# Fifteen seven-product pairs a layer, a middle convolution tap split between ScalarE and adding transfers, a down projection in four parts and a sixth split-weight slot, in a two-layer hybrid decoder on one core

## The chip, the cores and the metric

The kernel runs on one core of a Trainium2 chip. The metric is device time in microseconds (us), the median of several runs, lower is better. In the profile, PE is TensorE's matmul stream and PEld its weight loads, DVE is VectorE, ACT is ScalarE, POOL is GpSimd, and SP is the queue that issues most transfers. Lines are those of the kernel before; most instructions carry line 189, that of the helper through which all of them are recorded, so that groups are told apart by tile names.

## The reference, cut to what matters

Two layers (`DEPTH = 2`) over `x` of 512 tokens by 1024 channels, all in float32. Each layer mixes tokens (a convolution module, block-sparse attention and gated linear attention, side by side, under one input projection `w_in` and one output projection `w_out`), and then runs a gated MLP with a causal convolution of width 3 inside it:

```python
h = rms_norm(x, norm_ffn_g[l])                                  # 512 x 1024
u = causal_depthwise_conv(h @ ffn_w_up[l], ffn_conv_w[l], ffn_conv_b[l])   # 512 x 5632
x = x + (jax.nn.silu(u[..., :2816]) * u[..., 2816:]) @ ffn_w_down[l]       # 2816 -> 1024
```

The change lies almost wholly in this MLP. The output is `rms_norm(x, final_g)`.

## The kernel before

**How a product is done.** Activations lie transposed: 128 channels on the partitions, 512 tokens along them, so `x_sb[m]`, m = 0 to 7, are eight tiles of 128x512. A float32 product is made of three matmuls of split operands (`mm3`, line 458): high by high, high by low, low by high. Weights come raw from memory (`wraw`, issued by `dma_piece`, line 347, on SP, with three raw buffers), and are split on the chip by `split_piece` (line 367): ACT copies the rounded high part to `whi`, DVE subtracts it to give `wlo`. Split weights lie in `NWB = 5` slots of 1088 columns, and `ahead` (line 433) begins the split of up to two pieces beyond the one in use.

**The MLP.** The 2816 hidden channels are 22 blocks of 128, j = 0 to 21; for each j there is a block of the gate half (half 0, which goes through silu) and one of the other (half 1). Up projections come in two kinds. An "up" unit makes one block of one half: 24 matmuls of 128x512. A "pair" (`pair_unit`, line 508) makes both blocks of one j at once, over token halves, by seven products in place of eight (Strassen's scheme in Winograd's form): 84 matmuls of 128x256, and in return sums of weights (`sums`, line 389, inside `split_piece`: four DVE additions, two more half-size splits) and six additions or copies of half tiles when the PSUM banks are emptied (`ffn_pair`, line 1474). The sums of activations that all pairs share are made once a layer (`operand_sums`, line 1522). `PAIRS` (line 59) names the j that are pairs: 8 to 21 without 15, thirteen a layer.

**The convolution.** `taps` (line 1448) takes a block `u` that lies in a padded buffer: ACT writes `t = u * fw(2) + bias`, DVE adds `u` shifted by one times `fw(1)`, then `u` shifted by two times `fw(0)`; for half 0 ACT applies silu; when both halves are there DVE multiplies them, and the product is split again into the operands `gT_[j]` of the down projection. The padded buffers come from `take_pad` (line 1429), which has POOL clear two columns first.

**The down projection** sums over the 22 blocks in `PARTS = [8, 8, 6]`: each part is eight units m = 0 to 7, each of 3 matmuls per block of the part. The result of a part that isn't the last goes through `residual_job` (line 781): ACT copies the PSUM bank into a temporary `t`, and POOL issues a transfer that adds it to `x_sb[m]` (`x<-t`, line 787). The last part ends the layer, and is added by DVE.

**What sets the order.** The program is one hand-run schedule. `ffn_plan` (line 70) lists the MLP's units: for each j two "up"s or one "pair", and `DPER = 2` down units after each j from the point where their part is due. All other work (splits, convolutions, evictions) is written as generators (`Job`), which yield the tiles that they wait for; `tick`, called between the matmuls, runs a job's next step when a `Clock` with a cost for each engine says that what it needs is ready, and `force` runs jobs until a condition holds. Each engine then takes its instructions in the order in which they were so emitted. A transfer that adds is given a fixed delay in this clock, before what it writes counts as ready (`DLAT = 8000`, in ns):

```python
nc.gpsimd.dma_start(out=x_sb[m], in_=t, accum_op=ALU.add)
clk.ready[key(x_sb[m])] = max(clk.ready.get(key(x_sb[m]), 0.0), clk.t["PE"]) + DLAT
```

The vb projection, by `unit_tok` (line 556), is the one place where activations are the stationary operand and weights, 272 columns wide, stream; its weights came in two pieces of 1088 columns. `gate` is a 96x512 pattern of ones and zeros, built once by POOL at the start (lines 671 and 677), and `columns` (line 772) makes a column of scales for the vb rows, using the identity `ident`.

Of the kernel before, what the change touches and what calls it, by code (L numbers as in the profile page):

```python
# [8 lines left out]
F32 = mybir.dt.float32  # L9
# [8 lines left out]
P = 128  # L18
# [9 lines left out]
PARTS = [8, 8, 6]  # L28
OFFS = [0, 8, 16]
VBW = 272  # L30
WSLOT = 4 * VBW
# [13 lines left out]
TB = 48  # L45
# [11 lines left out]
NWB = 5  # L57
H = S // 2
PAIRS = [j for j in range(8, 22) if j != 15]
DPER = 2  # L60
NRAWJ = 3
DLAT = 8000.0
Q = 4 * P
# [131 lines left out]
def trunk(ctx, tc, xT, wg, wi, wvb, wc, wo, wug, wuh, wu, ws, wdg, wd, cols, gatew, fing, outT):  # L195
# [119 lines left out]
    for l in range(DEPTH):  # L315
        pieces += [(wg[l, i], 2 * GW) for i in range(4)]
        tok = 0
        for names in PLAN[1:]:
            if names[0] == "vb":
                pieces += [(wvb[l, i], 4 * VBW) for i in range(2)]  # L320
            elif names[0] in WIDE:
                pieces += [(wc[l, tok + i], 2 * S) for i in range(4)]
                tok += 4
            else:
                pieces += [(wi[l, UNITS.index(names[0])], KD * P)]
        pieces += [(wo[l, i], KD * P) for i in range(8)]
        pieces += [(wug[l, i], 2 * GW) for i in range(4)] + [(wu[l, i], KD * P) for i in range(2 * NRAWJ - 3)]
        pieces += [(wuh[l, i], 2 * GW) for i in range(4)] + [(wu[l, 2 * NRAWJ - 3], KD * P)]
        nu = 2 * NRAWJ - 2
        for what, a, b in FFN:  # L330
            if what == "up":
                pieces += [(wu[l, nu], KD * P)]
                nu += 1
            elif what == "pair":
                i = PAIRS.index(a)
                pieces += [(ws[l, i, 0], 2 * Q, "first"), (ws[l, i, 1], 2 * Q, "second")]
            elif what == "down":
                o, n = OFFS[a], PARTS[a]
                pieces += [(wd[l, b, :, o * P:(o + n) * P], n * P)]
        o, n = OFFS[-1], PARTS[-1]  # L340
        pieces += [(wdg[l, :, a * GW:b * GW], (b - a) * GW) for a, b in pairs(n)]
        pieces += [(wd[l, m, :, o * P:(o + n) * P], n * P) for m in range(3, KD)]
    st = {"next": 0, "dma": 0, "split": 0, "live": 0, "held": 0, "q": 1}
    raws, loaded = {}, {}
    AHEAD = 2
# [87 lines left out]
    def ahead():  # L433

        while st["split"] < min(len(pieces), st["next"] + AHEAD):
            if st["live"] + (2 if pieces[st["split"]][2:] == ("second",) else 1) > NWB:
                break
            split_piece()
# [69 lines left out]
    def pair_unit(B, on_done):  # L508
# [11 lines left out]
        st["held"] += 2  # L520
        k4 = lambda t: t.rearrange("p (k c) -> p k c", c=P)
# [34 lines left out]
    def unit_tok(lhs, w, on_done):  # L556

        ws = get(2)
        hs = [a.rearrange("p (k c) -> p k c", c=w) for a, _ in ws]
        ls = [b.rearrange("p (k c) -> p k c", c=w) for _, b in ws]  # L560
        for tb in range(NT):
            ps = PM()
            sl = slice(tb * P, (tb + 1) * P)
            for k in range(KD):
                mm3(ps[:, :w], lhs[k][0][:, sl], lhs[k][1][:, sl], hs[k // 4][:, k % 4, :],
                    ls[k // 4][:, k % 4, :], k == 0, k == KD - 1)
            post(on_done(tb, ps), ps)
# [68 lines left out]
    ones = const.tile([P, P], F32, name="ones")  # L636
    V.memset(ones, 1.0)
    mean_f = const.tile([P, P], F32, name="mean_f")
# [11 lines left out]
    ident = const.tile([P, P], F32, name="ident")  # L650
    nc.gpsimd.memset(ident, 0.0)
    nc.gpsimd.affine_select(out=ident, in_=ident, compare_op=ALU.not_equal, fill=1.0, base=0,
                            pattern=[[-1, P]], channel_multiplier=1)
    identr = const.tile([P, P], F32R, name="identr")
    nc.gpsimd.tensor_copy(out=identr, in_=ident)
    cmaskf = const.tile([P, P], F32, name="cmaskf")
# [13 lines left out]
    gate_0 = const.tile([96, S], F32, name="gate_0")  # L670
    nc.gpsimd.memset(gate_0, 0.0)

    def gate_weights():
        yield lambda: max(2e4, clk.ready.get(key(gw_sb), INF))
        A.activation(gate_w.rearrange("p l c -> p (l c)"), gate_0, AF.Copy)
        for r in (16, 80):
            nc.gpsimd.affine_select(out=gate_0, in_=gate_0, compare_op=ALU.not_equal, fill=1.0, base=-r,
                                    pattern=[[0, S]], channel_multiplier=1)
# [120 lines left out]
    def last_blocks(ks):  # L799
# [23 lines left out]
        def half(m, hs):  # L823
            def f(ps):
# [14 lines left out]
                if m + 2 == KD:  # L839
                    yield [acc, 1]  # L840
                    stat[hs.start] = PX()
                    PE.matmul(stat[hs.start][:, :H], mean_f, acc[:, hs], start=True, stop=False)
                yield [sq]
                PE.matmul(stat[hs.start][:, :H], mean_f, sq[:, :H], start=False, stop=m + 1 == KD)
# [200 lines left out]
    def gla_gates(l, vb, kT, qT, res, flags, qbd):  # L1045
# [6 lines left out]
        A.activation(gT[:96], gate_0, AF.Copy)  # L1052
# [208 lines left out]
    for l in range(DEPTH):  # L1261
# [186 lines left out]
        def taps(half, j, u):  # L1448
# [5 lines left out]
                             bias=col_sb[:, l, C_FB + cj:C_FB + cj + 1])  # L1454
                yield [t]
                V.scalar_tensor_tensor(t, u[:, 1:1 + S], fw(1), t, op0=ALU.mult, op1=ALU.add)
                V.scalar_tensor_tensor(t, u[:, 0:S], fw(0), t, op0=ALU.mult, op1=ALU.add)
                pads["n"] += 1
# [114 lines left out]
        ks = lambda pi: gT_[OFFS[pi]:OFFS[pi] + PARTS[pi]]  # L1573
        for what, i, m in FFN:
# [4 lines left out]
            else:  # L1579
                unit(ks(i), res(i, m))  # L1580
        if l + 1 == DEPTH:
            last_blocks(ks(last))
            break
# [7 lines left out]
def _layout(x, norm_mix_g, w_in, conv_w, conv_b, conv_ln_g, conv_ln_b, moba_out_g,  # L1591
# [18 lines left out]
    wvb = np.concatenate(parts(vbw, 4), axis=1)  # L1610
# [51 lines left out]
```

## Time and profile before

| | |
|---|---|
| median of 3 runs | 1129.82 us (1129.62 to 1130.07) |
| profiled execution, its own time | 1129.47 us |
| span in that execution | 1127.8 us |
| mean granted TensorE clock, of full speed | 0.997 |
| busy share of the span: PE, DVE, ACT, POOL | 99%, 82%, 57%, 6% |
| mean traffic over the span | 106 GB/s |

The span is the time from the first to the last instruction on the core; 1.67 us of the execution lie around it. Shares of busy time are means over the span. A matmul's duration in the rows is longer than the distance from one to the next, since they are pipelined; what a stretch costs is read from starts. A row of a timeline that ends in x2 stands for two instructions in a row, and its time is that of both.

### The profile page before, as it was taken

What the parts mean: (1) busy time and instruction counts of PE and PEld (TensorE: products, weight loads), DVE (VectorE), ACT (ScalarE), POOL (GpSimd) and SP (SyncE); (2) the same over time, 40 slices, a digit from 0 to 9 for tenths busy, and PEclk for the clock granted to TensorE, in tenths of its full rate; (3) what the DMA queues carried; (4) which work ended last, traced back from release to release, by engine and by line L of the source; (5) the groups of instructions that cost most, each with busy time, mean ns of one, the idle gap of its engine ahead of it and who ended that gap; (6) DMA issues with size and microseconds to landing.
All of it is one profiled execution on the core that took longest, in us unless ns stands there. A gap on an engine that the chain in (4) does not pass through costs nothing.

```text
span 1127.8 us, 17164 instructions
## 1 busy us (share of the span) xinstructions
PE 1116.4 (99%) x6582; PEld 972.3 (86%) x6582; DVE 921.0 (82%) x1489; ACT 640.7 (57%) x1016; POOL 67.8 (6%) x181
## 2 busy tenths in 40 slices
PE   9999999999999999999999999999999999999996
PEld 6988888888899899998888878888889899999886
DVE  7998866799987789767779979567999878996764
ACT  7465764667554555544554576446666554564554
POOL 2000102000000000100000011010000010000000
PEclk9999999999999999999999999999999999999998
DMA  7322227233254433453332212262323354244432
GB/s 238 97 74 74 63 66 156 87 98 98 71 143 119 110 115 112 124 152 92 119 115 75 75 57 75 76 137 92 108 94 107 100 132 137 88 125 137 99 108 75
DMA packets 40036, 119.00 MB, mean 106 GB/s; under 512 B 4609, under 2 KB 6913, under 8 KB 39954
## 3 DMA queue, kind: packets, MB, share of 16 engines
q1 hardware_dynamic: 32210, 104.53, 29.8%
q0 software_dynamic: 6912, 12.59, 6.4%
q8 instruction: 51, 0.84, 0.3%
q10 hardware_dynamic: 832, 0.79, 0.2%
q14 instruction: 31, 0.25, 0.1%
HBM read 103.21 MB, written 2.10 MB: 93 GB/s over the span
## 4 chain that ended last, share of the span: by engine, by line
PE 98%; ACT 1%; DVE 0%; DMA 0%; issue 0%; ACTq 0%; DVEq 0%
PE pm L189 82%; PE px L189 16%; ACT t L189 0%; DMA g_sb<-in_dram 0%; DVE t L189 0%; ACT x L189 0%; DVE wlo L189 0%; ACT whi L189 0%; DVE x L189 0%; ACTq L611 0%; DVEq L1657 0%; DVEq L189 0%; ACTq L189 0%
## 5 line engine op out<-in xcount | busy, mean ns | idle before, releaser
L189 PE MATMUL pm<-t,whi 128*128 128x512 f32 (+1 forms) x2476 | 685.8, 362 | 0.8 <-ACT t L189 0.8
L189 PEld LDWEIGHTS pm<-t,whi 128*128 128x128 f32 x2476 | 441.0, 189 | 71.1 <-ACT t L189 1.6
L189 PE MATMUL pm<-t,wlo 128*128 128x512 f32 (+1 forms) x1238 | 443.7, 360 | 0.4 <-DVE wlo L189 0.4
L189 DVE TENSOR_TENSOR wlo<-wraw,whi 128x1024 fp32r<-128x1024 f32 (+4 forms) x229 | 252.6, 1109 | 61.6 <-ACT whi L189 61.3
L189 PEld LDWEIGHTS pm<-t,wlo 128*128 128x128 f32 x1238 | 233.7, 189 | 36.3 <-DVE wlo L189 0.9
L189 ACT ACTIVATE whi<-wraw 128x1024 fp32r<-128x1024 f32 (+3 forms) x227 | 218.8, 968 | 57.1 <-DMA wraw<-in_dram 32.2
L189 ACT ACTIVATE t<-t 128x512 f32<-128x512 f32 (+3 forms) x220 | 133.0, 618 | 151.9 <-DVE t L189 150.3
L189 DVE TENSOR_TENSOR t<-t 128x512 f32<-128x512 f32 (+3 forms) x219 | 139.7, 651 | 18.8 <-ACT t L189 16.5
L189 DVE SCALAR_TENSOR_TENSOR t<-u,col_sb,t 128x512 f32<-128x512 f32 x176 | 129.9, 749 | 14.5 <-ACT t L189 10.5
L189 PE MATMUL pm<-bop,whi 128*128 128x256 f32 x516 | 96.7, 283 | 0.0
L189 ACT ACTIVATE t<-u,col_sb 128x512 f32<-128x512 f32 x88 | 68.9, 809 | 34.4 <-DVE u L189 33.9
L189 DVE SCALAR_TENSOR_TENSOR t<-hp,col_sb,t 128x512 f32<-128x512 f32 x120 | 82.6, 744 | 2.8 <-issue 2.3
L189 PEld LDWEIGHTS pm<-bop,whi 128*128 128x128 f32 x516 | 80.5, 192 | 0.0
L189 PE MATMUL pm<-bop,wlo 128*128 128x256 f32 x258 | 73.2, 284 | 0.0
L189 PE MATMUL px<-t,whi 128*128 128x512 f32 (+1 forms) x244 | 73.1, 374 | 0.0
L189 ACT COPY t<-pm 128x512 f32<-128x512 f32 x70 | 40.5, 578 | 49.8 <-PE pm L189 49.3
L787 POOL DMA_DIRECT2D x<-t x48 | 41.9, 909 | 421.2 <-ACT t L189 372.0
L189 PE MATMUL pm<-whi,t 128*128 128x272 f32 (+1 forms) x224 | 59.3, 339 | 0.0
L189 PEld LDWEIGHTS px<-t,whi 128*128 128x128 f32 x244 | 44.6, 188 | 8.1
L189 PEld LDWEIGHTS pm<-bop,wlo 128*128 128x128 f32 x258 | 49.5, 192 | 0.1
L189 ACT COPY u<-pm 128x256 f32<-128x256 f32 (+1 forms) x48 | 22.3, 465 | 44.5 <-PE pm L189 44.5
L189 ACT COPY t<-px 128x512 f32<-128x512 f32 (+2 forms) x50 | 24.5, 507 | 38.3 <-PE px L189 36.2
(158 smaller groups left out, 1144.4 us busy)
## 6 DMA issues: line engine op xcount, KB each, us to landing
wraw<-in_dram SPq DMA_DIRECT2D x158, 512.0 KB, 3.6
wraw<-in_dram SPq DMA_DIRECT2D x39, 384.0 KB, 3.3
x<-t POOLq DMA_DIRECT2D x48, 256.0 KB, 5.3
wraw<-in_dram SPq DMA_DIRECT2D x4, 544.0 KB, 3.8
x<-in_dram SPq DMA_DIRECT2D x7, 256.0 KB, 5.6
out_dram<-t SPq DMA_DIRECT2D x4, 256.0 KB, 2.3
out_dram<-t SPq DMA_DIRECT2D x4, 128.0 KB, 2.2
out_dram<-t ACTq DMA_DIRECT2D x2, 256.0 KB, 2.2
```

Of the source, the lines that this page charges most:

```text
L189: return real(*a, **k)
L787: nc.gpsimd.dma_start(out=x_sb[m], in_=t, accum_op=ALU.add)
```

## The change

- `PAIRS` becomes j = 7 to 21, fifteen a layer (7 and 15 are new).
- The down projection has four parts, of 5, 5, 6 and 6 blocks.
- For j = 3 to 20 the middle tap leaves DVE: ACT writes `mid = u * fw(1)` of the shifted block into another temporary, DVE does the tap `fw(0)` first, and then POOL issues a transfer that adds `mid` to `t` (line 1468 of the changed kernel), after which `t` counts as ready 6000 ns later (`TLAT`). What read `t` before (silu, or the product) now waits for that transfer.
- There are six split-weight slots, of 1024 columns; in the MLP `ahead` looks three pieces ahead, and a pair calls it once more at its start. For this the vb weights come in three pieces (816, 816 and 544 columns), and small constants move into temporaries: the identity is used through its rounded copy, and the gate pattern is made by POOL anew in each layer (`gate_pattern`, a memset and two selects).

```diff
-PARTS = [8, 8, 6]
-OFFS = [0, 8, 16]
+PARTS = [5, 5, 6, 6]
+OFFS = [0, 5, 10, 16]
 VBW = 272
-WSLOT = 4 * VBW
+WSLOT = KD * P
+VPARTS = ((0, 3), (3, 6), (6, 8))
...
-TB = 48
+TB = 47
...
-NWB = 5
+NWB = 6
 H = S // 2
-PAIRS = [j for j in range(8, 22) if j != 15]
+PAIRS = [j for j in range(7, 22)]
 DPER = 2
 NRAWJ = 3
 DLAT = 8000.0
+TLAT = 6000.0
+TAPJ = range(3, 21)
...
-                pieces += [(wvb[l, i], 4 * VBW) for i in range(2)]
+                pieces += [(wvb[l, :, a * VBW:b * VBW], (b - a) * VBW) for a, b in VPARTS]
...
-        while st["split"] < min(len(pieces), st["next"] + AHEAD):
+        while st["split"] < min(len(pieces), st["next"] + st["ahead"]):
...
         quads, _ = loaded.pop(i)
         st["held"] += 2
+        ahead()
...
-        ws = get(2)
+        ws = get(len(VPARTS))
...
+    def gate_pattern():
+        t = T()[:96]
+        nc.gpsimd.memset(t, 0.0)
+        for r in (16, 80):
+            nc.gpsimd.affine_select(out=t, in_=t, compare_op=ALU.not_equal, fill=1.0, base=-r,
+                                    pattern=[[0, S]], channel_multiplier=1)
+        return t
...
         gT = T(F32R)
-        A.activation(gT[:96], gate_0, AF.Copy)
+        A.activation(gT[:96], gate_pattern(), AF.Copy)
...
                 A.activation(t, u[:, 2:2 + S], AF.Identity, scale=fw(2),
                              bias=col_sb[:, l, C_FB + cj:C_FB + cj + 1])
+                if j in TAPJ:
+
+                    mid = T()
+                    A.activation(mid, u[:, 1:1 + S], AF.Copy, scale=fw(1))
                 yield [t]
-                V.scalar_tensor_tensor(t, u[:, 1:1 + S], fw(1), t, op0=ALU.mult, op1=ALU.add)
                 V.scalar_tensor_tensor(t, u[:, 0:S], fw(0), t, op0=ALU.mult, op1=ALU.add)
+                if j in TAPJ:
+                    yield [t, mid]
+                    nc.gpsimd.dma_start(out=t, in_=mid, accum_op=ALU.add)
+                    clk.ready[key(t)] = max(clk.ready[key(t)], clk.t["PE"]) + TLAT
+                else:
+                    V.scalar_tensor_tensor(t, u[:, 1:1 + S], fw(1), t, op0=ALU.mult, op1=ALU.add)
...
         ks = lambda pi: gT_[OFFS[pi]:OFFS[pi] + PARTS[pi]]
+        st["ahead"] = 3
         for what, i, m in FFN:
...
+        st["ahead"] = 2
```

In the built program the change has 6428 matmul instructions where there were 6284, 136 transfers on POOL's queue where there were 48, and 239 on SP's where there were 221. Since the emitted order follows the clock, it also moves instructions. Three places of it follow; names are those of the buffers, with their numbers left out unless they tell rows apart.

**DVE at the first layer's vb projection** (`wlo` are split weights, `hp` the padded inputs of the convolution module, `rb` and `rcol` the norm's scales). Before:

```order
L189 TENSOR_TENSOR wlo<-wraw,whi 128x1088
L189 TENSOR_TENSOR hp<-pm,rb 128x512
L189 TENSOR_TENSOR t<-pm,rb 128x512
L189 TENSOR_TENSOR hp<-pm,rb 128x512
L189 TENSOR_TENSOR t<-rb,ident 128x512
L189 TENSOR_REDUCE rcol<-t 128x4
L189 TENSOR_TENSOR t<-px,rb 128x512
L189 TENSOR_TENSOR hp<-hp,t 128x512
L189 TENSOR_TENSOR wlo<-wraw,whi 128x1024 x2
```

and in the change:

```order
L192 TENSOR_TENSOR wlo<-wraw,whi 128x816
L192 TENSOR_TENSOR hp<-pm,rb 128x512
L192 TENSOR_TENSOR t<-pm,rb 128x512
L192 TENSOR_TENSOR hp<-pm,rb 128x512
L192 TENSOR_TENSOR t<-rb,identr 128x512
L192 TENSOR_REDUCE rcol<-t 128x4
L192 TENSOR_TENSOR t<-px,rb 128x512
L192 TENSOR_TENSOR hp<-hp,t 128x512
L192 TENSOR_TENSOR wlo<-wraw,whi 128x544
L192 TENSOR_TENSOR wlo<-wraw,whi 128x1024 x2
```

The first `wlo` is here the last of the two vb pieces before and the second of three in the change; the low part of the third piece (544 columns) now stands behind `hp<-hp,t`, seven instructions later than the last vb piece stood.

**POOL in the middle of the first layer's pairs** (`x_NN<-t` adds a down projection's result, `t<-t` a middle tap; the memsets are those of the padded buffers). Before:

```order
L787 DMA x_89<-t 128x512
L787 DMA x_90<-t 128x512
L1432 MEMSET u 128x2 x2
L787 DMA x_91<-t 128x512
L787 DMA x_92<-t 128x512
```

and in the change:

```order
L792 DMA x_91<-t 128x512
L1468 DMA t<-t 128x512
L792 DMA x_92<-t 128x512
L1468 DMA t<-t 128x512
L1437 MEMSET u 128x2 x2
L792 DMA x_93<-t 128x512
L1468 DMA t<-t 128x512
L792 DMA x_94<-t 128x512
L1468 DMA t<-t 128x512
```

A transfer of a tap now follows each one of a result; between two pairs there are four in place of two.

**ACT at a pair's first eviction** (`t<-pm 128x512` is the copy of the pair's first PSUM bank, `t<-u,col_sb` a tap, `whi` and `qhi` split weights), here at the pair j = 17. Before:

```order
L189 COPY u<-pm 128x256
L189 ACTIVATE qhi<-wraw 128x512
L189 ACTIVATE t<-u,col_sb 128x512
L189 COPY t<-pm 128x512
L189 ACTIVATE whi<-wraw 128x1024
L189 ACTIVATE t<-u,col_sb 128x512
```

and in the change, at the same pair:

```order
L192 COPY u<-pm 128x256
L192 ACTIVATE qhi<-wraw 128x512
L192 ACTIVATE whi<-wraw 128x1024
L192 ACTIVATE t<-u,col_sb 128x512 x2
L192 COPY t<-pm 128x512
L192 ACTIVATE t<-t 128x512
L192 ACTIVATE t<-u,col_sb 128x512 x2
```

Ahead of the copy stood a half-size split and one tap; now a split of 1024 columns and two taps (the outer and the middle one of a block) stand between that half-size split and the copy.

## Rows read from the trace of the kernel before

**Rows 1.** Page part 1: busy us, share of the span, instructions by engine.
```profile
PE 1116.4 (99%) x6582; PEld 972.3 (86%) x6582; DVE 921.0 (82%) x1489; ACT 640.7 (57%) x1016; POOL 67.8 (6%) x181
```

**Rows 2.** Page part 4: the chain that ended last, its shares by engine.
```profile
PE 98%; ACT 1%; DVE 0%; DMA 0%; issue 0%; ACTq 0%; DVEq 0%
```

**Rows 3.** Waits of PE, whole span: us in total, times, longest us.
```profile
PE pw L627 <- DVE zerob L189: 1.1, 1, 1.1
PE pm L189 <- ACT t L189: 0.8, 1, 0.8
```

**Rows 4.** Timeline of PE around j = 15 and 16: start, us, instruction.
```profile
413.57 0.63 PE L189 MATMUL pm<-t,whi 128*128 128x512 f32 x2
...
424.48 0.40 PE L189 MATMUL pm<-t,whi 128*128 128x256 f32 x2
...
434.55 0.40 PE L189 MATMUL pm<-t,whi 128*128 128x256 f32 x2
```

**Rows 5.** Timeline of PE in the second pair, j = 9.
```profile
310.68 0.39 PE L189 MATMUL pm<-bop,wlo 128*128 128x256 f32 x1
310.90 0.40 PE L189 MATMUL pm<-bop,whi 128*128 128x256 f32 x2
```

**Rows 6.** Groups by form, 195:553: count, busy us, mean ns, idle before.
```profile
L189 DVE SCALAR_TENSOR_TENSOR t<-u,col_sb,t 128x512 f32<-128x512 f32 x88 | 64.9, 749 | 7.2 <-ACT t L189 5.2 <-issue 0.3
L189 ACT ACTIVATE whi<-wraw 128x1024 fp32r<-128x1024 f32 x54 | 56.9, 1054 | 27.6 <-DMA wraw<-in_dram 15.2 <-DVE wraw L189 11.6 <-PE pm L189 0.7
L189 ACT ACTIVATE t<-u,col_sb 128x512 f32<-128x512 f32 x44 | 34.5, 809 | 17.1 <-DVE u L189 16.9
L189 DVE TENSOR_TENSOR wraw<-wraw 128x512 f32<-128x512 f32 x26 | 17.9, 688 | 2.0 <-DMA wraw<-in_dram 1.6
L189 ACT COPY t<-pm 128x512 f32<-128x512 f32 x29 | 16.7, 577 | 19.4 <-PE pm L189 19.4
L189 ACT ACTIVATE t<-x,col_sb 128x512 fp32r<-128x512 f32 x13 | 9.4, 722 | 18.8 <-DVE x L189 18.8
L189 DVE TENSOR_TENSOR u<-t,pm 128x256 f32<-128x256 f32 x13 | 5.4, 412 | 0.2
```

**Rows 7.** Windows: stretch, length, busy PE, PEld, DVE, ACT, POOL, clock, DMA share.
```profile
438.00:523.00 85.00, 85.00 (x539) 77.42 (x538) 65.18 (x98) 43.84 (x65) 7.61 (x18) 1.00 0.47 125
...
sum 358.00, PE 357.98 PEld 318.47 DVE 298.55 ACT 202.90 POOL 17.36; mean PE 89.50 PEld 79.62 DVE 74.64 ACT 50.72 POOL 4.34
```

**Rows 8.** Timeline of PE at the first layer's vb projection.
```profile
29.55 0.28 PE L189 MATMUL pm<-whi,t 128*128 128x272 f32 x1
...
31.94 0.29 PE L189 MATMUL pm<-wlo,t 128*128 128x272 f32 x1
```

**Rows 9.** Timeline of DVE at the same place.
```profile
31.22 0.68 DVE L189 TENSOR_TENSOR hp<-hp,t 128x512 f32<-128x512 f32 x1
```

**Rows 10.** Line 787, the 48 adding transfers of `x<-t`.
```profile
DMA to landing us min/median/max: 3.3/5.3/8.1
```

**Rows 11.** Transfers issued in 389.5:394: KB each, median us to landing.
```profile
x<-t POOLq DMA_DIRECT2D x1, 256.0 KB, 3.3
```

**Rows 12.** Transfers issued in 394:397.
```profile
wraw<-in_dram SPq DMA_DIRECT2D x1, 512.0 KB, 7.1
x<-t POOLq DMA_DIRECT2D x1, 256.0 KB, 7.4
```

**Rows 13.** Page part 3, SP's and POOL's queues: packets, MB, share of 16 engines.
```profile
q1 hardware_dynamic: 32210, 104.53, 29.8%
q0 software_dynamic: 6912, 12.59, 6.4%
```

**Rows 14.** Waits of ACT, 300:520.
```profile
ACT whi L189 <- DMA wraw<-in_dram: 15.2, 11, 3.1
```

**Rows 15.** Groups of POOL, whole span.
```profile
L677 POOL TENSOR_SCALAR_AFFINE_SELECT gate<-gate 96x512 f32<-96x512 f32 x2 | 3.0, 1485 | 16.6 <-ACT gate_w L189 16.6
```

**Rows 16.** Waits of POOL, whole span.
```profile
POOL t L1101 <- PE px L189: 149.2, 2, 141.9
```

More of the change, by code (lines that the diff above doesn't have):

```diff
@@ L342, in trunk @@
         pieces += [(wd[l, m, :, o * P:(o + n) * P], n * P) for m in range(3, KD)]
-    st = {"next": 0, "dma": 0, "split": 0, "live": 0, "held": 0, "q": 1}
+    st = {"next": 0, "dma": 0, "split": 0, "live": 0, "held": 0, "q": 1, "ahead": 2}
     raws, loaded = {}, {}
-    AHEAD = 2
     def dma_piece():
@@ L556, in unit_tok @@
     def unit_tok(lhs, w, on_done):
-        ws = get(2)
-        hs = [a.rearrange("p (k c) -> p k c", c=w) for a, _ in ws]
-        ls = [b.rearrange("p (k c) -> p k c", c=w) for _, b in ws]
+        ws = get(len(VPARTS))
+        wk = [tuple(t[:, (k - a) * w:(k - a + 1) * w] for t in hl) for hl, (a, b) in zip(ws, VPARTS) for k in range(a, b)]
         for tb in range(NT):
@@ L564, in unit_tok @@
             for k in range(KD):
-                mm3(ps[:, :w], lhs[k][0][:, sl], lhs[k][1][:, sl], hs[k // 4][:, k % 4, :],
-                    ls[k // 4][:, k % 4, :], k == 0, k == KD - 1)
+                mm3(ps[:, :w], lhs[k][0][:, sl], lhs[k][1][:, sl], wk[k][0], wk[k][1], k == 0, k == KD - 1)
             post(on_done(tb, ps), ps)
@@ L634, in trunk @@
         dma_piece()
-    ones = const.tile([P, P], F32, name="ones")
+    t0, t1 = T(), T()
+    ones, mean_f, ident0, cmaskf = t0[:, :P], t0[:, P:2 * P], t1[:, :P], t1[:, P:2 * P]
     V.memset(ones, 1.0)
-    mean_f = const.tile([P, P], F32, name="mean_f")
     V.memset(mean_f, -0.5 / D)
@@ L649, in trunk @@
     A.activation(warm, ones[:, 0:1], AF.Exp)
-    ident = const.tile([P, P], F32, name="ident")
-    nc.gpsimd.memset(ident, 0.0)
-    nc.gpsimd.affine_select(out=ident, in_=ident, compare_op=ALU.not_equal, fill=1.0, base=0,
+    nc.gpsimd.memset(ident0, 0.0)
+    nc.gpsimd.affine_select(out=ident0, in_=ident0, compare_op=ALU.not_equal, fill=1.0, base=0,
                             pattern=[[-1, P]], channel_multiplier=1)
     identr = const.tile([P, P], F32R, name="identr")
-    nc.gpsimd.tensor_copy(out=identr, in_=ident)
-    cmaskf = const.tile([P, P], F32, name="cmaskf")
+    nc.gpsimd.tensor_copy(out=identr, in_=ident0)
+    ident = identr.bitcast(F32)
     nc.gpsimd.memset(cmaskf, 0.0)
@@ L669, in trunk @@
     gate_w = const.tile([96, DEPTH, 256], F32R, name="gate_w")
-    gate_0 = const.tile([96, S], F32, name="gate_0")
-    nc.gpsimd.memset(gate_0, 0.0)
+    def gate_pattern():
[5 more added lines that the diff above has]
+        return t
     def gate_weights():
         yield lambda: max(2e4, clk.ready.get(key(gw_sb), INF))
[L675 to L678, printed above, removed]
+        z = T()[:96]
+        nc.gpsimd.memset(z, 0.0)
+        A.activation(gate_w.rearrange("p l c -> p (l c)"), z, AF.Copy)
         yield [gate_w]
@@ L841, in f @@
                     stat[hs.start] = PX()
-                    PE.matmul(stat[hs.start][:, :H], mean_f, acc[:, hs], start=True, stop=False)
+                    PE.matmul(stat[hs.start][:, :H], mean_d.bitcast(F32), acc[:, hs], start=True, stop=False)
                 yield [sq]
-                PE.matmul(stat[hs.start][:, :H], mean_f, sq[:, :H], start=False, stop=m + 1 == KD)
+                PE.matmul(stat[hs.start][:, :H], mean_d.bitcast(F32), sq[:, :H], start=False, stop=m + 1 == KD)
                 if m + 1 == KD:
@@ L1609, in _layout @@
     parts = lambda a, n: [a[:, :, n * i:n * i + n].reshape(L, 1, P, -1) for i in range(KD // n)]
-    wvb = np.concatenate(parts(vbw, 4), axis=1)
+    wvb = vbw.reshape(L, P, KD * VBW)
     wc = np.concatenate([p for a in (1792,) for p in parts(wk[..., a:a + S], 2)], axis=1)
```

## Prediction

> **What bounds the kernel now.** The first view is the page's busy times: PE is busy 99% of the span, DVE 82%, ACT 57%, POOL 6% [rows 1]. A mean says little about a stage, so the chain that ended last comes next: 98% of it is PE [rows 2]. Third are PE's own waits: the two longest are 1.1 and 0.8 us, once each [rows 3], both in the kernel's start. So what counts in the middle is how many matmuls PE issues and how far apart; what other engines do is free until a wait of PE appears. In the first layer's MLP, 195 to 553 us, the windows give PE 357.98 busy of 358.00, DVE 298.55 and ACT 202.90 [rows 7].
>
> **Two pairs a layer in place of four "up" units.** In the timeline of PE the two "up"s of j = 15 run from 413.57 to 424.48, 10.91 us for 48 matmuls of 512 columns, 0.227 apart; the pair after them runs to 434.55, 10.07 us for 84 of 256 columns, 0.120 apart [rows 4]. A pair saves 0.84 us, four of them **3.4 us**. Nothing hides this, since PE is the bound; it is lost only where PE begins to wait. PE also hesitates in the second pair: 310.68 to 310.90 is 0.22 us where 0.12 is the step [rows 5]; four such places, of 0.10 to 0.18, make 0.5 us in the first two pairs, where weight sums or the bank's copy come late. The additional call of `ahead` starts those sums earlier. I take them as gone, **-0.5**; bounds -0.7 and +0.3, the latter if they only move to the new first pair, j = 7.
>
> **Taps.** Per layer 36 DVE instructions of 0.749 go, 27.0 us; 36 scalings by ACT come, for which the nearest row without a bias is 0.722 [rows 6], 26.0 us. The fourth part brings eight more copies by ACT, 8 x 0.577 = 4.6 us, and eight more adding transfers. For two pairs more DVE has eight sums of 0.688, six half-size subtractions of about that, a 1024-column one as in an "up" and ten half-tile operations of 0.412 [rows 6], some 11 us with small change; ACT 1 us. So ACT goes from 203 to about 235 us of 358 (66%), DVE from 299 to about 283 (79%). Neither becomes the bound, and what is saved on DVE is worth nothing by itself.
>
> **Transfers.** The 48 adds of before took 6.4% of sixteen engines' span [rows 13], 72 us, 1.5 us each. A layer has 44 more: 66 us on 358, 18 points; the highest share of DMA in a stretch was 0.47 [rows 7], so it stays near 0.65. The loads have slack: ACT waited for raw weights 11 times between 300 and 520, up to 3.1 us [rows 14], with PE untouched. Issuing them is POOL's work, which is busy 17 of 358 us [rows 7].
>
> What counts is when the result of a tap arrives. An add of 256 KB landed 3.3 to 8.1 us after issue, median 5.3 [rows 10]: 3.3 with little else under way [rows 11], 7.4 beside a load of 512 KB which itself took 7.1 [rows 12]. In the changed order I count the PE work between each tap transfer's place and its first reader's, at 0.120 and 0.227 a matmul: 4.1 to 10.7 us over the 72 transfers, median 7.4. Eleven have under 5.5. Seven of these block ACT before silu, where the next thing that PE needs lies 5.8 us or more ahead of its use. The other four block DVE's product (pairs j = 7 and 13 of each layer; the POOL order above shows the second place, x_91 and x_92, with two adds and two taps in four consecutive issues). There the reader stands 4.7 us behind the transfer; a pair's eviction stands 4.4 us behind the reader on DVE, and PE needs its bank 2.7 us after that eviction's place. With some 0.4 us from place to issue, PE waits landing minus (4.7 + 2.7 - 0.4), that is **landing - 7.0**, at each. At the median, and up to 7.0, it is nothing; at 7.4 it is 0.4. I take +0.3 for the four together; the ends are 0 (all at 5.3) and 4 x 1.1 = 4.4 (all at 8.1).
>
> For such a transfer the Trainium skill, "DMA: Bandwidth & Descriptors", section "Anatomy of one DMA — SWDGE (gpsimd) path", fits 2.0 us plus bytes over 436e3, which is 2.6 us for 256 KB; no row here is that short. By it every tap would be in place before its reader and the sum would be 0.3 us better than mine.
>
> **The vb weights in three pieces.** PE starts the first vb block at 29.55, and its twentieth matmul, the first to need the low part of the third piece, at 31.94 [rows 8]. In the change that low part stands on DVE behind the instruction that runs from 31.22 to 31.90 [rows 9]; 544 columns take some 0.7, so it ends near 32.5, 0.6 late. An earlier subtraction is shorter (816 columns, not 1088), which gives back up to 0.3. **+0.4**, between 0.2 and 0.6; the second layer has room there.
>
> **The copy of a pair's first bank at j = 17.** ACT has after the half-size split a split of 1.054, two taps of 0.809 and 0.722 and the copy of 0.577 [rows 6], 3.2 us, while PE has 24 matmuls of 0.120, 2.9 us, before it needs the bank. **+0.3** in each layer, between 0 (the split starts earlier) and 0.7 (the taps wait for their block).
>
> **The rest.** The gate pattern costs POOL two selects of 1.485 [rows 15] and a memset; POOL waits 149.2 us around its work there [rows 16], which hides them; if POOL were late, 3.5 us at most would be exposed once a layer. Shorter slots, a sixth slot, a third piece ahead and the shared constants issue no work on PE; their cover is the loads' slack above.
>
> **Sum:** -3.4 - 0.5 + 0.4 + 0.6 + 0.3 = -2.6 us. The profiled execution took 1129.47 and would take 1126.9; the median of before stands 0.35 above it, so the forecast is 1127.2. 0.2% is 2.26 us, about what a measurement of this kernel can tell from no change, so "faster" begins at 1127.56.
>
> **The rivals.**
> 1. *Everything fits.* The taps land near 5 us, the copies at j = 17 are covered: -3.4 - 0.5 + 0.2 = -3.7, 1126.1. For it: the median landing, ACT's 66%. Against it: the adds of before that met a load took 7.4.
> 2. *The gain is eaten.* Landing is about 7.5 at the four places (2.0 us), the first-pair hesitations stay and the copies cost 0.5 each: -3.4 + 0.4 + 1.0 + 2.0 = 0.0, 1129.8. For it: rows 12 show 7.4 with one add and one load, and here more come together.
> 3. *Slower: the taps arrive late.* At the middle of the pairs two adds and two taps are issued within 4 us beside up to three loads. At 1.5 us each the four take 6 us of all engines, and three loads of 512 KB about 5 more (104.53 MB of loads took 29.8% of the span [rows 13], 1.7 us for each 512 KB): 11 us of work for what must be there after 7.0. If the last of them lands at 8.5, each place costs 1.5 us: 6.0, and some 0.8 at the seven ACT readers, less 2.9 for the rest: +3.9, 1133.7. It decides where landing passes 7.6 or so. For it: the longest landing of before, 8.1 [rows 10], with a third of the transfers. Against it: only two places a layer are this tight, and the loads run ahead, so that they need not fall just there. On this the Trainium skill, same page, section "Queues, rings and completion order", says that each engine alternates between the queues that have work, packet by packet. By that a tap is slowed by a load and doesn't queue behind all of it; rows 12, where add and load end together, agree.
> 4. *The pairs don't save.* If the weight pieces of fifteen pairs came late, PE would wait for splits: two raw pieces are read per pair as before for two "up"s, so only a slower load could do it; 1 us at each of four new pairs gives +1.4, 1131.2. ACT's unpunished waits [rows 14] speak against it.
>
> **How the numbers follow.** Forecast 0.50, of which 0.40 below 1127.56 and 0.10 above; rival 1, 0.12; rival 2, 0.18; rival 3, 0.16; rival 4, 0.04. Faster 0.52, same 0.28, slower 0.20. The forecast's own range is 1125.9 to 1128.3: the terms at their better ends make -3.9, and at the worse ones not all meet. The range of 8 in 10 begins at 1125.6, a little below for a hesitation more that goes, and reaches to 1132.5, over rivals 2 and 4 and the milder half of rival 3.
>
> **What would show it.** PE's starts: pairs at j = 7 and 15 of 10.1 us. PE's waits: at most 0.6 us on a low split near 32, some tenths on ACT's copy at j = 17. Taps: landing with a median between 5 and 7 us, DVE's product released by a transfer at some of the four places, with PE's step after it unbroken. ACT about 66% and DVE 79% busy in the MLP. The prediction is wrong if PE waits for DVE's evictions a few us after taps that land beyond 7.0, if silu on ACT holds up a split, or if raw weights arrive too late for the pairs.

## The result, and the profile after

The change makes the kernel slower: median 1162.12 us (1158.33 to 1163.54) beside 1129.91 for the kernel before, ratio 1.028 with a 95% interval of 1.0267 to 1.0293. The profiled execution took 1163.54, its span is 1161.8 us, 34.0 more than before.

The page of the changed kernel: busy time by engine (part 1), the two queues (part 3: packets, MB, share of sixteen engines) and the chain (part 4). They answer to [rows 1], [rows 13] and [rows 2].

```profile
PE 1125.6 (97%) x6726; PEld 982.5 (85%) x6726; DVE 894.8 (77%) x1483; ACT 692.4 (60%) x1134; POOL 146.5 (13%) x273
...
q1 hardware_dynamic: 34802, 104.53, 28.0%
q0 software_dynamic: 19584, 35.66, 17.9%
...
PE 54%; issue 13%; DMA 13%; DVE 12%; ACT 6%; POOL 2%; SPq 0%; DVEq 0%; POOLq 0%; ACTq 0%
```

PE issues 6726 matmul records in place of 6582, as planned, but it no longer makes up the chain: 98% became 54%, and transfers, DVE and ACT have the rest. DVE, the busiest engine behind PE and its weight loads, fell from 82% to 77%, so by these means over the span no other engine has more to do than it can; the engines stand waiting for one another. Next the waits (us in total, times, longest us) of PE, then those of DVE and ACT for transfers, and last ACT's for raw weights before (line 189); they answer to [rows 3] and [rows 14].

```profile
PE pm L192 <- DVE u L192: 9.4, 5, 4.7
PE pm L192 <- ACT t L192: 6.7, 4, 3.2
PE pm L192 <- DVE t L192: 6.0, 4, 2.1
PE pm L192 <- DVE wlo L192: 2.1, 3, 1.2
PE px L192 <- DVE t L192: 1.2, 1, 1.2
...
DVE t L192 <- DMA t<-t: 42.3, 13, 7.8
...
ACT whi L192 <- DMA wraw<-in_dram: 68.8, 40, 3.6
...
ACT t L192 <- DMA t<-t: 19.7, 7, 5.2
```

```profile
ACT whi L189 <- DMA wraw<-in_dram: 32.2, 23, 3.1
```

Apart from the 1.1 us at the very start, PE waits 25.4 us here where it waited 1.2 (0.8 and 0.4). Behind most of it stand two kinds of late transfers: DVE waits 42.3 us and ACT 19.7 us for taps (`t<-t`), and ACT 68.8 us for raw weights, where it was 32.2 us over the whole span before.

**How one wait grows.** The place that the prediction named, x_91 and x_92 and two taps, between 412 and 432 us. First POOL's timeline (start, us, instruction, idle before), then DVE's, then PE's, and the windows around the wait (columns as in [rows 7]: the clock stands behind POOL's busy time).

```profile
413.08 0.86 POOL L792 DMA_DIRECT2D x<-t  x1 [14.51 <-ACT t L192]
414.41 0.86 POOL L1468 DMA_DIRECT2D t<-t  x1 [0.47 <-DVE t L192]
415.64 0.86 POOL L792 DMA_DIRECT2D x<-t  x1 [0.37 <-issue]
416.22 1.17 POOL L1468 DMA_DIRECT2D t<-t  x1
```

```profile
418.90 0.42 DVE L192 TENSOR_TENSOR t<-pm,t 128x256 f32<-128x256 f32 x1
427.14 0.69 DVE L192 TENSOR_TENSOR t<-t 128x512 f32<-128x512 f32 x1 [7.81 <-DMA t<-t]
...
430.74 0.41 DVE L192 TENSOR_TENSOR u<-t,pm 128x256 f32<-128x256 f32 x1
```

```profile
426.15 0.39 PE L192 MATMUL pm<-t,wlo 128*128 128x512 f32 x1
431.20 1.22 PE L192 MATMUL pm<-t,whi 128*128 128x512 f32 x2 [4.66 <-DVE u L192]
```

```profile
420.00:426.00 6.00, 6.00 (x40) 5.47 (x40) 0.00 (x0) 0.63 (x1) 0.00 (x0) 1.00 0.78 188
426.00:430.90 4.90, 0.54 (x3) 0.12 (x1) 3.69 (x7) 1.88 (x4) 0.00 (x0) 1.00 0.01 2
430.90:434.20 3.30, 3.00 (x7) 2.45 (x8) 3.30 (x7) 3.30 (x7) 0.00 (x0) 0.51 0.00 0
```

The chain gives the tap of 416.22 as 10.82 us under way, to 427.04. DVE had nothing to do from 419.3, but its next instruction multiplies with that tap, so it stood 7.81 us; behind it came a few sums of weights and then the eviction of the pair's bank at 430.74, for which PE waited 4.66. After the wait PE's granted clock is 0.51 for 3.3 us, its lower level of 1.2 GHz: matmuls step by 0.43 us where 0.227 is usual. It fell so behind five of PE's waits, for 3.4 us each time, and not behind the others. Counted over the trace from 195 us on, steps without a wait of their own that are over 1.6 times the usual one cost 11.4 us, 3.2 before. With the waits (24.2 more) and the pairs (3.4 less) that makes 29 of the 34 us; the other 5 I put down to what lies around each wait, some 0.1 to 0.2 us for the step itself, and to smaller hesitations.

What was issued in that stretch, 412 to 430 us (KB each, median us to landing), answers to [rows 12]:

```profile
wraw<-in_dram SPq DMA_DIRECT2D x3, 512.0 KB, 6.0
x<-t POOLq DMA_DIRECT2D x2, 256.0 KB, 7.7
t<-t POOLq DMA_DIRECT2D x2, 256.0 KB, 9.9
```

Over the whole trace these were the landings of the 72 taps:

```profile
DMA to landing us min/median/max: 3.2/4.8/10.8
```

The middle lies under that of [rows 10], 5.3, and the worst ones lie well over 8.1.

### The profile page after: what moved, and what is told of

Its sections match the earlier page's. It is cut to its first block, busy times and chain, and to the rows that moved or that the text cites. A ratio compares the mean times of both kernels' runs of the same rounds, so it can differ in the third digit from the quotient of the medians.

```text
span 1161.8 us, 17785 instructions
## 1 busy us (share of the span) xinstructions
PE 1125.6 (97%) x6726; PEld 982.5 (85%) x6726; DVE 894.8 (77%) x1483; ACT 692.4 (60%) x1134; POOL 146.5 (13%) x273
## 3 DMA queue, kind: packets, MB, share of 16 engines
q0 software_dynamic: 19584, 35.66, 17.9%
## 4 chain that ended last, share of the span: by engine, by line
PE 54%; issue 13%; DMA 13%; DVE 12%; ACT 6%; POOL 2%; SPq 0%; DVEq 0%; POOLq 0%; ACTq 0%
PE pm L192 41%; PE px L192 12%; DMA t<-t 8%; DVE t L192 6%; DMA wraw<-in_dram 5%; ACT t L192 3%; DVE wlo L192 3%; DVE wraw L192 2%; ACT whi L192 2%; POOL t L1468 1%; POOL x L792 1%; DVE u L192 1%; DVE qlo L192 0%; ACT qhi L192 0%; POOL u L1437 0%
## 5 line engine op out<-in xcount | busy, mean ns | idle before, releaser
L192 PEld LDWEIGHTS pm<-t,whi 128*128 128x128 f32 x2456 | 436.6, 191 | 80.0 <-DVE u L192 11.8
L192 DVE TENSOR_TENSOR wlo<-wraw,whi 128x1024 fp32r<-128x1024 f32 (+6 forms) x251 | 257.8, 1033 | 81.7 <-ACT whi L192 81.0
L192 ACT ACTIVATE whi<-wraw 128x1024 fp32r<-128x1024 f32 (+4 forms) x249 | 224.0, 907 | 117.8 <-DMA wraw<-in_dram 68.8
L192 ACT ACTIVATE t<-t 128x512 fp32r<-128x512 f32 (+3 forms) x222 | 134.2, 617 | 150.4 <-DVE t L192 129.1
L192 DVE TENSOR_TENSOR t<-t 128x512 f32<-128x512 f32 (+3 forms) x219 | 140.8, 652 | 70.2 <-DMA t<-t 42.3
L192 PE MATMUL pm<-bop,whi 128*128 128x256 f32 x648 | 121.8, 284 | 5.9 <-DVE t L192 5.7
L192 ACT ACTIVATE t<-u,col_sb 128x512 f32<-128x512 f32 x160 | 115.1, 765 | 14.2 <-DVE u L192 13.9
L192 PEld LDWEIGHTS pm<-bop,whi 128*128 128x128 f32 x648 | 101.0, 192 | 6.9 <-DVE t L192 6.9
L1468 POOL DMA_DIRECT2D t<-t x72 | 66.0, 923 | 316.7 <-ACT t L192 126.6
L192 PE MATMUL pm<-bop,wlo 128*128 128x256 f32 x324 | 91.7, 283 | 0.0
L192 DVE SCALAR_TENSOR_TENSOR t<-u,col_sb,t 128x512 f32<-128x512 f32 x104 | 77.1, 746 | 4.7 <-ACT t L192 3.9
L192 PE MATMUL pm<-t,qhi 128*128 128x256 f32 x240 | 47.0, 294 | 6.7 <-ACT t L192 6.7
```

The costliest lines, as they stand in the source:

```text
L192: return real(*a, **k)
L1468: nc.gpsimd.dma_start(out=t, in_=mid, accum_op=ALU.add)
```

## The experiments

Medians are beside the kernel before as run on the same chips: 1129.5 to 1129.9. The question was first which part of the change costs the 32 us.

**Round one: undo one part, or do one alone.**

The taps back on DVE (`e1`):
```diff
-TAPJ = range(3, 21)
+TAPJ = ()
```


> The changed kernel with the middle tap back on DVE (no tap transfers; fifteen pairs, four parts, six slots kept). Theory A (the taps' transfers land 8 to 11 us after issue where two of them, two adds and two or three loads are issued within 4 us, and stop DVE's and ACT's queues): PE's waits on DVE and ACT fall from 25 us to under 3, and the time is 1126 to 1128. Rival B (fifteen pairs with three pieces ahead ask too much of ACT, DVE and the raw loads, for which ACT waits 68.8 us): 1145 or more. Rival C (the fourth part's sixteen further adds fill POOL's queue and the DMA engines): 1140 or more.

Measured: 1147.35 us, ratio 1.0152 [1.0136, 1.0168]. Theory A's 1126 to 1128 is a miss, and the number alone fits rivals B and C as well as it fits two causes: 14.8 us go, 17.5 stay, and ACT still waits 68.1 us for raw weights.

Only the taps, on the kernel before (`e2`; lines of `taps` as in the change):
```diff
+TLAT = 6000.0
+TAPJ = range(3, 21)
```


> The kernel before with nothing but the middle tap by ACT and an adding transfer, j = 3 to 20, counted ready after 6000 ns (thirteen pairs, three parts, five slots). Theory A: slower than before by 15 to 35 us, 1145 to 1165, with DVE waiting for t<-t. Rival B or C: the taps alone cost little, 1129 to 1134.

Measured: 1129.48, ratio 0.9995 [0.9986, 1.0005]: no change. Theory A as it stood falls: taps by transfer cost nothing in the kernel before, with its three parts, thirteen pairs and five slots. There they land in 3.4 us in the median and 6.0 at most.

The readers moved away from the taps (`e3`):
```diff
-TLAT = 6000.0
+TLAT = 12000.0
```


> The changed kernel with the tap counted as ready 12000 ns after its place in place of 6000 (its first reader then stands 7.5 to 16.9 us of PE work behind, median 13.7, where it stood 4.1 to 10.7). Nothing else is changed, and the same transfers and loads run. Theory A (the reader stands too near): most of PE's waits go, 1128 to 1138. Rival D (the traffic itself: loads and adds slow each other so that raw weights come late, wherever the readers stand): 1150 or more. Rival B or C: 1150 or more.

Measured: 1148.72, ratio 1.0168 [1.0152, 1.0184]. With the same transfers PE no longer waits for evictions by DVE (`DVE u`), and 13.4 us go, nearly what leaving out the taps brought. So the taps' part of the loss is the distance of their readers, not their traffic. The rest is something else that remains with and without taps; rival B's strain on the raw loads is nearest to it, though B forecast 1150 or more. PE's waits for results of ACT and DVE in `e3`:

```profile
PE pm L192 <- ACT t L192: 11.1, 9, 3.4
...
PE pm L192 <- DVE t L192: 1.0, 3, 0.4
```

Three parts (`e4`):
```diff
-PARTS = [5, 5, 6, 6]
-OFFS = [0, 5, 10, 16]
+PARTS = [8, 8, 6]
+OFFS = [0, 8, 16]
```


> The changed kernel with the down projection in three parts (8, 8, 6) again: 48 adds in place of 64, taps kept. Readers stand 5.3 to 11.8 us behind their transfer. Theory A: the bursts of two adds and two taps remain where down units run, fewer of them and with readers a little further: 1138 to 1158. Rival C (the further adds): back to about 1128. Rival B: 1155 or more.

Measured: 1134.35, ratio 1.004 [1.0025, 1.0055]. 27.8 us of 32 go with the fourth part, more than theory A gave and less than rival C's 1128. Taps land within 7.5 us here, median 3.7, and their readers stand 5.3 to 11.8 us behind them, not 4.1 to 10.7; the run doesn't tell the two apart.

**Round two: the fourth part and the pairs.**

Thirteen pairs in the change (`e5`):
```diff
-PAIRS = [j for j in range(7, 22)]
+PAIRS = [j for j in range(8, 22) if j != 15]
```


> The changed kernel with thirteen pairs a layer (j = 8 to 21 without 15), all else kept. Theory E (a pair asks DVE for 12 to 14 us in its 10.1 us of PE and is paid for by the down units and the ups between pairs; four parts make those units 3.4 us in place of 5.4, and j = 15 no longer pays): most of what is left without the late taps goes, 1134 to 1146. Theory A alone (late taps, in the same bursts): still 1142 or more. Rival D (traffic, 64 adds and 72 taps): 1150 or more.

Measured: 1150.72, ratio 1.0188 [1.0173, 1.0203]; without the two pairs a layer, 11.4 of the 32 us go. That is a miss for theory E; theory A alone and rival D both allow it.

Four parts alone on the kernel before (`e6`):
```diff
-PARTS = [8, 8, 6]
-OFFS = [0, 8, 16]
+PARTS = [5, 5, 6, 6]
+OFFS = [0, 5, 10, 16]
```

> The kernel before with only the down projection in four parts (5, 5, 6, 6), so thirteen pairs, taps on DVE, five slots. Theory E: DVE's surplus isn't paid back between the pairs, 1135 to 1150. Rival G (the pairs at 7 and 15 are to blame and the parts harmless): 1129 to 1132.

Measured: 1163.81, ratio 1.0303 [1.0288, 1.0319]: alone the fourth part is as bad as the whole change, beyond both ranges. But PE waits for other things than in the change: nearly all of it is a pair's second product, whose weights are the first split of the weight sums (high part `whi`, then low part `wlo`).

```profile
PE pm L189 <- DVE wlo L189: 13.5, 14, 1.3
PE pm L189 <- ACT whi L189: 5.9, 11, 1.0
```

A fourth raw buffer, with five split slots for room (`e7`; the first loads are issued to match):
```diff
-NRAW = 3
+NRAW = 4
...
-NWB = 6
+NWB = 5
```


> The changed kernel with four raw weight buffers in place of three and five split slots in place of six. Rival F (the raw buffers are what the loop of load, ACT and DVE runs out of): 1145 or less, ACT's waits for raw loads (68.8 us) under half. Theory E (DVE's surplus and late taps): 1154 to 1165, the waits for loads turn into waits for DVE.

Measured: 1150.33, ratio 1.0186 [1.0169, 1.0203], between the two. ACT's waits for raw weights are all but gone (0.4 us); what PE waits for most is 10.8 us of evictions, and in front of them DVE waits 48.1 us for taps.

Taps and fifteen pairs, three parts, five slots (`e8`, on `e2`):
```diff
-PAIRS = [j for j in range(8, 22) if j != 15]
+PAIRS = [j for j in range(7, 22)]
```

> The kernel before with the taps by ACT and transfer and fifteen pairs, three parts, five slots, two pieces ahead. Theory E: the long down units pay, and the taps relieve DVE: 1126 to 1131. Rival G (the pairs at 7 and 15 are to blame): 1134 or more. It also tells what six slots and three pieces ahead are worth beside the run with three parts, 1134.35.

Measured: 1137.24, ratio 1.0071 [1.0056, 1.0086]. A miss for theory E, and within rival G's range: beside `e2` the two pairs a layer cost 7.8 us here. PE waits 9.7 us for the low part of the first split sums (`wlo`), as in `e6`. `e4`, which has the same parts, pairs and taps with six slots and three pieces ahead, is 2.9 us faster.

**Round three: two causes?**

Both remedies (`e9`, on `e7`):
```diff
-TLAT = 6000.0
+TLAT = 12000.0
```

> The changed kernel with both the fourth raw buffer (and five split slots) and the tap counted as ready after 12000 ns; four parts and fifteen pairs kept. Theory H (two causes that add: the taps' readers stand too near, worth 13 us; and three raw buffers can't cycle four pieces in the 16.9 us of a pair with two short down units, where load and hold take 15 to 18 us a buffer and three allow 12.7, worth 12 us): both go, 1134 to 1141. Rival E (DVE has more work than the pairs leave it time for, whatever the buffers): 1145 or more. Rival I (one cause seen from two sides, a late transfer that also keeps a raw buffer): about as either alone, 1147 to 1150.

Measured: 1129.46, ratio 0.9997 [0.9988, 1.0006]. Better than their sum, and outside all three ranges; the whole loss is gone, with four parts and fifteen pairs in place. ACT has no wait for raw weights left.

Four raw buffers without taps (`e10`, on `e7`):
```diff
-TAPJ = range(3, 21)
+TAPJ = ()
```

> The changed kernel with four raw buffers, five slots and the taps back on DVE. Theory H: 1147.35 less some 10 us, 1133 to 1141. Rival E (DVE's surplus, which is greatest here, 15.3 us of DVE in 16.9): 1145 or more, with DVE over 90% busy between 300 and 400 us.

Measured: 1130.67, ratio 1.0008 [0.9999, 1.0017]. Better than theory H, and against E: DVE has its taps back and is 87% busy between 300 and 400 us, and there is almost no loss.

Three parts and 9000 ns (`e11`, on `e7`):
```diff
-PARTS = [5, 5, 6, 6]
-OFFS = [0, 5, 10, 16]
+PARTS = [8, 8, 6]
+OFFS = [0, 8, 16]
...
-TLAT = 6000.0
+TLAT = 9000.0
```

> The changed kernel with three parts (8, 8, 6), four raw buffers, five slots and the tap counted as ready after 9000 ns; fifteen pairs. Theory H: the buffers' cycle and the readers both have room; only the pairs at 15 and 16, which follow one another with no down unit between, may wait: 1126 to 1131. Rival E: 1133 to 1137 as with three raw buffers (1134.35).

Measured: 1129.78, ratio 1.0 [0.9991, 1.0009], as theory H has it.

The same without the pair at 15 (`e12`):
```diff
-PAIRS = [j for j in range(7, 22)]
+PAIRS = [j for j in range(7, 22) if j != 15]
```


> The run before this one without the pair at 15 (fourteen pairs, j = 7 to 21 without 15). Theory H and theory E alike: no wait is left in the MLP, and two pairs of 0.84 us and the first pairs' hesitations come off the kernel before: 1127.0 to 1128.5. If the pair at 7 is itself too early for the weights: 1129 to 1132.

Measured: 1131.71, ratio 1.0014 [1.0005, 1.0022], a miss: small waits at the vb projection, at the first pair (0.4 us on `qlo`, in each layer) and a start that is 1.0 us later in the trace ate the pairs' gain. It doesn't tell against the pair at 15: beside `e11` the run is 1.9 us slower, near the 1.7 us that two pairs save.

**Round four: slots or raw buffers?** `e7`, `e9` and `e10` had changed both.

Five slots and three raw buffers (`e13`, on `e3`):
```diff
-NWB = 6
+NWB = 5
```

> The changed kernel with the tap counted as ready after 12000 ns and five split slots in place of six, three raw buffers as in the change. Theory H (three raw buffers are the limit): 1140 or more, ACT still waiting over 30 us for raw loads. Rival J (it was the sixth slot, which lets splits run into one another, and not the raw buffers, that the runs with four buffers and five slots did away with): 1129 to 1132.

Measured: 1131.69, ratio 1.0015 [1.0006, 1.0025]. Theory H falls and rival J is right, with the taps in time: taking away the sixth slot alone brings 17.0 us here, the fourth raw buffer another 2.2. ACT's waits for raw weights in the change, in `e3` and in `e13`:

```profile
ACT whi L192 <- DMA wraw<-in_dram: 68.8, 40, 3.6
```
```profile
ACT whi L192 <- DMA wraw<-in_dram: 42.4, 25, 3.0
```
```profile
ACT whi L192 <- DMA wraw<-in_dram: 16.3, 13, 3.7
```

The emitted order suggests why. From 300 to 520 us, the PE work between a raw load's place and that of its first reader has a median of 8.8 us before, 4.4 in the change, 5.7 in `e3`, 7.0 in `e13` and 12.7 in `e9`. A free slot lets a split be written as soon as the planner's clock thinks its load has come; between 300 and 520 us of the changed kernel a load took 4.3 us in the median and up to 8.7, and ACT, which takes its instructions in order, stands in front of it with evictions and taps behind. That the slot costs 17.0 us is measured; that this is the way in which it costs them is argued from these distances and ACT's waits.

Two pieces of vb weights again, on `e9` (`e14`):
```diff
-WSLOT = KD * P
-VPARTS = ((0, 3), (3, 6), (6, 8))
+WSLOT = 4 * VBW
+VPARTS = ((0, 4), (4, 8))
```


> The changed kernel with four raw buffers, five slots, the tap counted as ready after 12000 ns, and the vb weights in two pieces of 1088 columns as before. Theory H and the prediction's step on vb: the wait near 32 us goes, 0.5 us less than 1129.46, so 1128.6 to 1129.4. If the wait there has another cause: 1129.5.

Measured: 1127.10, ratio 0.9974 [0.9965, 0.9984], more than expected, 2.4 us less than `e9`: besides the wait near 32 us those of 0.2 us at the start of both MLPs went, and some other hesitations of PE.

The kernel before with four parts and four raw buffers (`e15`, on `e6`; two temporaries fewer for room):
```diff
-TB = 48
+TB = 46
...
-NRAW = 3
+NRAW = 4
```

> The kernel before with the down projection in four parts (1163.81 with three raw buffers) and four raw buffers, with two temporaries fewer for room; thirteen pairs, five slots, taps on DVE. Theory H: the loss goes here too, 1129 to 1136. Rival J or E (PE waits for the first split of a pair because five slots leave no room to split ahead, or because DVE has no time): 1150 or more.

Measured: 1159.74, ratio 1.0263 [1.0249, 1.0277]. Raw buffers don't help the kernel before with four parts; PE still waits 13.2 us for the low part of the first split sums. That is a third way to lose, which the change doesn't show. It looks two pieces ahead where the change looks three, and I take that for the cause, but the look-ahead was not tried alone.

A delay between (`e16`, on `e7`):
```diff
-TLAT = 6000.0
+TLAT = 9000.0
```

> The changed kernel with four raw buffers, five slots and the tap counted as ready after 9000 ns (first readers 5.7 to 14.5 us behind, where 6000 gave 1150.33 and 12000 gave 1129.46). Theory A's part (PE waits landing less the reader's distance less what DVE's next eviction can bear): some readers of a burst that lands at 8 to 11 us are still too near, 1130 to 1138. If only the 4 to 6 us places hurt: 1129.5.

Measured: 1128.44, ratio 0.9988 [0.9979, 0.9997]. Theory A's part is a miss: three thousand ns more than the change allows are enough, 21.9 us beside `e7`, although taps land nearly as late as there, where it was up to 10.9:

```profile
DMA to landing us min/median/max: 3.2/6.0/10.3
```

**Round five: the missing corner, and the best.**

The change with five slots only (`e17`):
```diff
-NWB = 6
+NWB = 5
```

> The changed kernel with five split slots in place of six and nothing else (taps ready after 6000 ns, three raw buffers, 1024-column slots). It is the fourth corner beside the change (1162.12), the change with 12000 ns (1148.72) and with both (1131.69). Theory J2 (the sixth slot places ACT's splits too near behind their raw loads, median 4.4 us of PE work in place of 6.4 between 300 and 520 us, so that ACT stands before weights that have not landed; this adds to the late taps): 1143 to 1151, ACT's waits for raw loads under half of 68.8 us, PE's waits left on DVE's evictions. If the late taps alone make all of the loss as soon as they are there: 1155 or more.

Measured: 1167.45, ratio 1.0334 [1.0315, 1.0353]: a miss, and the theory that the two causes add falls with it. ACT's waits for raw weights fell below half, as theory J2 has it, and its splits stand 6.4 us behind their loads and no longer 4.4, and yet the kernel is 5.3 us slower than the change, in the range of late taps alone. PE's waits for evictions and ACT's for raw weights:

```profile
PE pm L192 <- DVE u L192: 14.3, 9, 3.7
```
```profile
ACT whi L192 <- DMA wraw<-in_dram: 32.4, 24, 3.1
```

| tap ready after | six slots, 3 raw | five slots, 3 raw | five slots, 4 raw |
|---|---|---|---|
| 6000 ns | 1162.12 | 1167.45 | 1150.33 |
| 9000 ns | not run | not run | 1128.44 |
| 12000 ns | 1148.72 | 1131.69 | 1129.46 |
| taps on DVE | 1147.35 | not run | 1130.67 |

Six slots with four raw buffers were not run. With late taps the sixth slot makes no loss that could be taken away; PE waits for evictions in either case (14.3 us, nine times, with five slots). Without them it costs 17.0. Each fault alone is worth 17 us or more, and with both there the one hides part of the other, so the 32 us cannot be shared out between them. The raw buffers are not harmless either: beside late taps and five slots the fourth one brings 17.1 us (1167.45 to 1150.33), and 2.2 where the taps are in time. Why late taps and three raw buffers hurt each other no run shows.

The pieces together (`e18`, on `e14`, so with four raw buffers, five slots and two vb pieces):
```diff
-TLAT = 12000.0
+TLAT = 9000.0
```

> The best of the pieces together: the change with four raw buffers, five slots, the tap ready after 9000 ns and the vb weights in two pieces. With 12000 ns this gave 1127.10; 9000 was 1.0 us better than 12000 with three vb pieces. Theory: 1126.0 to 1127.5, faster than both kernels. If the two gains are the same one: 1127.1 to 1128.4.

Measured: 1126.61 (1126.08 to 1126.91), ratio 0.9972 [0.9962, 0.9983]: faster than both kernels. Its page and the waits of PE:

```profile
PE 1112.5 (99%) x6726; PEld 976.3 (87%) x6726; DVE 894.5 (80%) x1481; ACT 694.4 (62%) x1132; POOL 146.7 (13%) x273
```
```profile
PE pw L628 <- DVE zerob L192: 1.0, 1, 1.0
PE pm L192 <- DVE wlo L192: 0.8, 1, 0.8
PE pm L192 <- ACT t L192: 0.7, 1, 0.7
```

All three waits lie in the start; none is left in an MLP, and the span is 1124.5, 3.3 us under that of before, close to the four pairs' 3.4.

## Why the prediction was wrong, step by step

It said 1127.2, 1125.6 to 1132.5; the time is 1162.12. Two steps failed: the sixth slot, which it put at nothing, and the late taps, which it put at 0.3 us. Two of the signs that it named as speaking against it came: PE waits for evictions behind taps that land beyond 7.0, and raw weights that arrive too late.

- **The pairs, -3.4.** Right, but hidden: `e18` has all four and no waits, and its span is 3.3 us shorter, the net of these pairs and of some tenths either way. The stage sums hold too: windows of its MLP, 195 to 553, give DVE 286 and ACT 231 us busy where 283 and 235 were forecast, and a DMA share of 0.66 at the highest where I had 0.65.
- **The hesitations in the first pairs, -0.5.** Right as far as seen: of steps over 1.6 times the usual one the kernel before has four in its first pairs, between 310 and 319 us, and the changed kernel and `e18` have none between 285 and 326 us.
- **The vb weights, +0.4.** Right at its place, too small as a whole. PE's timeline of the changed kernel has the wait and its releaser, where two steps of together 0.25 take 0.61. But two pieces in place of three bring 2.4 us from `e9` to `e14` and 1.8 from `e16` to `e18`: by PE's starts `e16` is 0.3 us behind `e18` after this place, 0.9 at the start of the first MLP and 1.9 near the end, so the second layer didn't have the room that I gave it.

```profile
31.98 0.41 PE L192 MATMUL pm<-whi,t 128*128 128x272 f32 x2
32.59 0.39 PE L192 MATMUL pm<-wlo,t 128*128 128x272 f32 x1 [0.20 <-DVE wlo L192]
```

- **The late taps, +0.3: the mechanism right, the size off.** "PE waits landing minus 7.0" gives 3.8 us for the landing of 10.82 above, and 4.66 was measured; the place was the right one. At the four places the taps landed after 9.2, 10.8, 8.6 and 9.2 us, and PE waited 1.6, 4.7, 0 and 1.4 us for the evictions behind them, 7.7 together:

```profile
328.50 0.73 PE L192 MATMUL pm<-t,whi 128*128 128x512 f32 x2 [1.56 <-DVE u L192]
```
```profile
1000.87 0.73 PE L192 MATMUL pm<-t,whi 128*128 128x512 f32 x2 [1.44 <-DVE u L192]
```

I had put the landings a little over 7.0, from a median of 5.3 and a worst of 8.1 in a kernel with a third of the transfers, and bounded the four by 4.4 us together; one alone took more than that. ACT stood at just the seven places that I had counted, but DVE stood at 13 and not at four: I had looked at readers under 5.5 us, and taps that land after 7 to 11 us reach those beyond it. Rival 3 had the sum of work right (four transfers and three loads, 11 us), took a landing of 8.5 from it, and with 6.0 for the four places came near. Its 1133.7 was too low by 28 us: the other nine places, the lower clock behind five of PE's waits and the next point are not in it. No run splits the 28 us between them.
- **"The loads have slack": wrong, and the step that failed outright.** I costed the sixth slot, the third piece ahead and the additional `ahead` at nothing, with ACT's 15.2 us of harmless waits [rows 14] as their cover. With the taps in time, taking back the sixth slot alone brings 17.0 us (`e3` to `e13`); the third piece ahead and the additional call stay in `e13`, which is within 2 us of the kernel before. The cover was one of the old order, in which a split stood 8.8 us behind its load. The change moved the splits to 4.4 us, and used the cover up; that this is what the slot's 17.0 us consist of is argued, as said above. I counted the distance from place to reader for the taps, and not for the loads, which need the same.
- **The copy at j = 17, +0.3 a layer.** The right place for the wrong reason: PE waited there 2.5 us in one layer and 3.2 in the other. The split before the copy took its 1.06 us, but stood 3.08 us in front of a raw load that took 5.76. ACT's timeline:

```profile
458.14 0.63 ACT L192 ACTIVATE qhi<-wraw 128x512 fp32r<-128x512 f32 x1
461.85 1.06 ACT L192 ACTIVATE whi<-wraw 128x1024 fp32r<-128x1024 f32 x1 [3.08 <-DMA wraw<-in_dram]
```

- **The fourth part.** I saw in it eight copies and eight transfers. It also shortens a down unit from 24 matmuls to 15 or 18, 5.4 us to 3.4 or 4.1, and puts adds behind twelve j of a layer where there were eight. `e4` shows that without it most taps are in time again: DVE's waits for them fall from 42.3 to 7.8 us, the longest landing from 10.8 to 7.5 us. That four parts are not bad in themselves is shown by `e16` and `e18`, which have them.

## What to carry to other kernels

Where a planner writes in-order queues from a fixed delay for each transfer, that delay has to come near the worst landing of a burst and not the median: here, with four raw buffers and taps that landed in up to 10.3 us, a delay of 9000 ns lost nothing in the MLPs and 6000 lost 22 us. Count for every kind of transfer how much work lies between its place and its first reader's, before and after; a further buffer that only lets a reader be placed earlier can make a kernel slower, when the data doesn't come earlier too (six slots in place of five, 17.0 us with the taps in time). And two faults in such queues don't add: with the taps still late, taking that buffer away made the kernel 5.3 us slower.

## What the runs showed of the hardware that was not expected

The transfers of a burst did not share the time evenly. The four of 413.08 to 416.22 landed 5.0, 8.9, 10.3 and 10.8 us after issue; each adding transfer took 17.9% of 1161.8 us over 136, 1.5 us of all sixteen engines, as before, so the last of the four, with three loads of 1.7 us beside them, came as late as the work of all of them, some 11 us by this estimate. The shortest landing of a tap was 3.2 us. After PE's idle of 4.7 us the granted clock was 0.51 for 3.3 us, 1.2 GHz, before it was full again; five such stretches of 3.4 us lie in the trace between 195 and 1100 us.
